# A hybrid decoder layer with 32 experts: writes moved to GpSimd's queue, two more fixed experts, two layer norms and two embeddings moved

## The chip, the cores and the metric

The kernel runs on one core of one Trainium2 chip. The metric is the device time of one execution in microseconds, as the median of several runs. A core has five engines with instruction streams of their own: TensorE (PE in the profile, its weight loads PEld), VectorE (DVE), ScalarE (ACT), GpSimd (POOL) and SyncE (SP), which only issues transfers. SyncE, ScalarE and GpSimd issue DMAs, and 16 DMA engines carry them.

## What is computed

One layer on 512 tokens of width 2048, all in float32:

```python
z = x @ w_in + b_in
y = concat(s5_group(z[:, :1024]), conformer_conv_group(z[:, 1024:2048], z[:, 2048:])) @ w_o + b_o
h = layer_norm(ALPHA * x + y, ln1_g, ln1_b)
# experts: 4 groups of 8; the best group, and in it the best 2 experts of each token
g_p, g_idx = top_k(softmax(h @ w_rg + b_rg), 1)
e_val, e_idx = top_k((h @ w_re + b_re)[the 8 of group g_idx], 2)
w = softmax(e_val) * g_p
m = sum over a token's 2 experts of (silu(h @ w_gate[e]) * (h @ w_up[e]) * w) @ w_down[e]
h = layer_norm(ALPHA * h + m, ln2_g, ln2_b)
e = (p @ w_p) * sigmoid(h @ w_pg + b_pg)        # p: a second input, 512 x 256
out = layer_norm(ALPHA * h + e, ln3_g, ln3_b)
```

An expert has 6 MB of weights (2048 x 512 for gate and up, 256 x 2048 for down), so 32 experts have 201 MB.

## The kernel before

The program is written as straight Python that unrolls every loop. A planner (`schedule_with_timeline_sim=True`) then decides the order of the instructions on each engine: it simulates the engines, and whenever one is free gives it the ready instruction that stands earliest in the code. So an instruction that stands late can run early if it is ready in a gap. Engines then run their own stream strictly in that order. The planner also places the semaphores. For the transfers of SyncE and ScalarE together it has eight, used in turn; a transfer waits until the one that used its semaphore before it has landed. GpSimd's transfers have eight of their own.

Tokens are worked on in four tiles of 128 (`m`, `NT` = 4). The stages that matter here are these.

The *output projection* (line 880 on) makes `tt[m]`, a tile's 128 x 2048 sums, in four column blocks `c`. `evac` adds a block, takes its statistics, and `logits` transposes it and multiplies it with the routers' weights (lines 843 to 859). In the last block `finish(m)` (line 861) makes mean and 1/sigma of the tile, its router logits `lg[:, m]` (line 867), and, for all but the last tile, calls `normalize`: eight instructions on VectorE (lines 180 and 181) and the write of the tile to `h_dram` (line 877, ScalarE's queue). The last tile's `normalize` stands further down, behind the counts (line 961).

The *routing* (lines 915 to 1036) works on VectorE with small tiles: group and expert choice (to line 955), the tokens of each expert by matmuls with ones (lines 957 to 960), each expert's rank by its count (lines 973 to 979), each token's rank and position (`rtok`, line 991), a one-hot of positions (line 190, called from `slot_hot`), and from it the rows to gather (`sl0`, line 196) and the weights (`wt0`, line 203). Experts named in `FIXED` get the last ranks whatever their counts. `embedding(m, x)` (line 828) multiplies a tile of p with `w_p` and writes it to `p_dram` (line 841); its argument `x` only makes it wait for that tile. Before, `embedding(0)` waits for the last logits, `embedding(1)` for the largest overflow count and `embedding(2)` for `wt0`.

The *expert stage* (line 1046 on) goes through `GROUPS`. A group is one pass of 128 token slots: one to four experts, given by rank, share the slots in strips of 128, 64 or 32. For each group GpSimd gathers token rows from `h_dram` (`gather`), TensorE transposes them (`columns`), multiplies with gate and up in four quarters (`up`, line 1103), and with down in two halves (`down`, line 1123), and GpSimd scatters the result to `y_dram`. A quarter or half of an expert is one 1 MB load by `ring_load` (line 1065) into a ring of `NRING` = 17 slots: 15 tiles that are there from the start and, once `w_p` is no longer needed, the two `raw` buffers. An expert number that comes from the routing is read into a register of SyncE (line 1137); a fixed one is in the code. Group 0 is the fixed experts 0 and 31. Its 12 loads are issued first (`early`), then three loads of group 1, then the embedding of the last tile with its two buffers `pe` of which there is one at a time (lines 1171 to 1179), then two more loads of group 1 into the raw buffers. Then comes a branch for tokens that found no slot (line 1187, not taken here), at which every engine settles its semaphores, and then the other groups.

The *last stage* (line 1246 on) loads `w_pg`, adds the experts' rows from `y_dram` to `tt`, and makes the second and third layer norm and the gate with `p_dram`.

Of the kernel before, what the change touches and what calls it, by code (L numbers as in the profile page):

```python
# [8 lines left out]
FT = mybir.dt.float32  # L9
# [8 lines left out]
P = 128  # L18
# [8 lines left out]
NT = S // P  # L27
NE = 32
FH = 256
ALPHA = 2.0 ** 0.25  # L30
# [12 lines left out]
FIXED = (0, NE - 1)  # L43
GROUPS = [(64, [(30, 2), (31, 2)]), (128, [(0, 4)]), (32, [(2, 3), (13, 1)]), (128, [(1, 4)]),
# [10 lines left out]
def build(tc, I, out, dbg=None, stages=9):  # L55
# [582 lines left out]
    if True:  # L638
# [146 lines left out]
        with ExitStack() as s3:  # L785
# [42 lines left out]
            def embedding(m, x):  # L828
# [5 lines left out]
                for q in range(2):  # L834
                    pe_ = wB.tile([P, 2, 512], FT, name="pe", tag="wlo", bufs=4)
                    for c in range(2):
                        ps = bank("ops")
                        for k in range(2):
                            T.matmul(ps, pm[:, k], wps[q][:, k, c * 512:(c + 1) * 512], start=k == 0, stop=k == 1)
                        A.copy(pe_[:, c], ps)  # L840
                    A.dma_start(p_dram[m, 2 * q:2 * q + 2].rearrange("c p d -> p c d"), pe_)
# [19 lines left out]
            def finish(m):  # L861
                mean, rstd = ln_stats(op_, st1[m], "s")
                nm = op_.tile([P, 1], FT, name="nm", bufs=2)
# [4 lines left out]
                if m < NT - 1:  # L868
                    normalize(m, mean, rstd)
                return mean, rstd  # L870

            def normalize(m, mean, rstd):
# [4 lines left out]
                A.dma_start(h_dram[m * P:(m + 1) * P], tt[m])  # L877
                dump("h", tt[m], lambda d: d[m * P:(m + 1) * P])

            for c in range(4):  # L880
# [19 lines left out]
                else:  # L900
                    hls = [next(w_o) for q in range(2)]
                    for m in range(NT):
# [3 lines left out]
                        last = finish(m)  # L906
# [5 lines left out]
            embedding(0, lg[:, NT - 1, 0:1])  # L912
# [48 lines left out]
            normalize(NT - 1, *last)  # L961
# [29 lines left out]
            V.tensor_reduce(rtok, pt2, axis=AX.X, op=OP.add)  # L991
            by_place, pw = rp1.tile([P, 2 * NT, NP], FT), rp.tile([P, 2 * NT, NP], FT)
# [44 lines left out]
            embedding(1, cmax)  # L1037
            embedding(2, wt0[:, 0:1])
# [8 lines left out]
    if True:  # L1047
# [84 lines left out]
        def expert(i, j):  # L1132
            if i == 0:
                return slice(FIXED[j], FIXED[j] + 1)
# [13 lines left out]
        pm3 = ep.tile([P, 2, P], FT, name="pm3")  # L1148
        nc.sync.dma_start(pm3, I["pT"][:, :, (NT - 1) * P:])
        for m in range(NT):  # L1150
            A.mul(tt[m], tt[m], ALPHA)
# [3 lines left out]
        for i, (width, members) in enumerate(GROUPS):  # L1155
# [4 lines left out]
            for q in range(4):  # L1160
                up(gu, st, early[q] if i == 0 else ahead1[q] if i == 1 else loads(i, q), q)
# [3 lines left out]
            for q in range(2):  # L1165
                down(at, st, early[4 + q] if i == 0 else ahead1[4] if (i, q) == (1, 0) else loads(i, 4 + q), q, sl0[:, NGR + i:NGR + i + 1])
# [3 lines left out]
            ahead1 = [loads(1, q) for q in range(3)]  # L1170

            for q in range(2):
                pe_ = ep.tile([P, 2, 512], FT, name="pe")
                for c in range(2):
                    ps = bank("dps", 4)
                    for k in range(2):
                        T.matmul(ps, pm3[:, k], wps[q][:, k, c * 512:(c + 1) * 512], start=k == 0, stop=k == 1)
                    (A.copy if c else V.tensor_copy)(pe_[:, c], ps)
                A.dma_start(p_dram[NT - 1, 2 * q:2 * q + 2].rearrange("c p d -> p c d"), pe_)
            ring.extend(rpool.tile([P, D], FT, name="raw", tag="raw", bufs=2) for _ in range(2))  # L1180
            ahead1 += [loads(1, q) for q in range(3, 5)]
# [282 lines left out]
```

## Time and profile before

| what | us |
|---|---|
| median of 3 runs (1479.26 to 1485.14) | 1480.44 |
| the profiled execution, whole | 1482.75 |
| its span, first to last instruction | 1480.9 |
| TensorE busy | 1262.3 (85%) |
| VectorE busy | 778.5 (53%) |
| ScalarE busy | 372.5 (25%) |
| GpSimd busy | 382.7 (26%) |

The mean granted TensorE clock was 0.926. 349.34 MB went through the DMA, 236 GB/s over the span. The profile gives, for one execution, each instruction with its start, its duration and what ended the idle time before it; DMA packets; and a chain of waits followed back from the last instruction. Times are from the span's start. "q" behind an engine's name marks its sequencer, which waits, branches and issues transfers.

### The profile page before, as it was taken

How to read it: one execution, taken by the hardware profiler on the slowest of the kernel's cores; microseconds unless marked ns; L12 is line 12 of the kernel's file. 1: busy time of each engine (PE TensorE's matmuls, PEld its weight loads, DVE VectorE, ACT ScalarE, POOL GpSimd, SP SyncE). 2: the span in 40 equal slices, each digit the busy share in tenths (PEclk: the TensorE clock that was granted, in tenths of full speed). 3: DMA queues.
4: the chain of work that ended last, by engine and by line, in shares of the span. 5: the costliest groups of instructions: out<-in, count | busy, mean ns of one | idle time of the engine just before them, and what ended most of it. 6: DMA issues, size and time to landing. Idle time of an engine off the chain costs nothing. (4 is left out here: it accounts for less than half of the span.)

```text
span 1480.9 us, 16676 instructions
## 1 busy us (share of the span) xinstructions
PE 1262.3 (85%) x6206; PEld 805.9 (54%) x6207; DVE 778.5 (53%) x1251; ACT 372.5 (25%) x559; POOL 382.7 (26%) x313
## 2 busy tenths in 40 slices
PE   6999999998999999968598998777676775599996
PEld 4887877887777888844243332221111111388884
DVE  7999899879998653681111110000000006985467
ACT  4335565544433432031001110000000003023210
POOL 0367768673945300000001111000000005700000
PEclk9998999998999999978899999898899986699998
DMA  6344445445632351147799999999999986426413
GB/s 233 112 131 118 150 122 156 142 117 174 246 123 85 114 210 57 44 170 284 298 422 420 420 420 416 418 417 414 415 411 411 411 351 235 142 107 213 142 44 121
DMA packets 97769, 349.34 MB, mean 236 GB/s; under 512 B 29705, under 2 KB 43529, under 8 KB 62097
## 3 DMA queue, kind: packets, MB, share of 16 engines
q1 hardware_dynamic: 51152, 303.21, 52.7%
q10 hardware_dynamic: 40912, 28.20, 6.6%
q0 software_dynamic: 5616, 16.79, 2.9%
q8 instruction: 51, 0.84, 0.2%
q14 instruction: 38, 0.30, 0.1%
HBM read 323.30 MB, written 35.34 MB: 242 GB/s over the span
## 5 line engine op out<-in xcount | busy, mean ns | idle before, releaser
L1103 PE MATMUL gu<-ring,xt 128*32 128x512 f32 (+2 forms) x1144 | 237.9, 671 | 58.7 <-DMA ring<-w_gu 58.7
L236 DVE SCALAR_TENSOR_TENSOR cps<-hc,wdw,cps 128x512 f32<-128x512 f32 x232 | 174.5, 752 | 4.8
L1103 PEld LDWEIGHTS gu<-ring,xt 128*32 128x32 f32 (+2 forms) x1144 | 58.7, 127 | 200.2 <-issue 100.2
L100 PE MATMUL zp<-xh,whi 128*128 128x512 f32 x384 | 157.5, 411 | 11.3 <-ACT whi L79 10.2
L79 ACT CAST whi<-raw 128x1024 fp32r<-128x1024 f32 x116 | 119.5, 1049 | 169.7 <-PE zp L102 55.7
L102 PE MATMUL zp<-xh,wlo 128*128 128x512 f32 x384 | 155.2, 404 | 1.5 <-DVE wlo L80 1.5
L101 PE MATMUL zp<-xl,whi 128*128 128x512 f32 x384 | 154.9, 403 | 1.6 <-DVE xl L80 1.6
L80 DVE TENSOR_TENSOR wlo<-raw,whi 128x1024 fp32r<-128x1024 f32 x90 | 123.8, 1386 | 55.3 <-ACT whi L79 54.4
L1109 DVE TENSOR_TENSOR act<-act,gu 128x256 f32<-128x256 f32 x13 | 5.5, 421 | 268.9 <-ACT act L1108 268.9
L1123 PE MATMUL dps<-ring,at 128*32 128x512 f32 (+2 forms) x568 | 113.6, 612 | 12.1 <-DMA ring<-w_dn 7.0
L1073 POOL DMA_INDIRECT y_dram<-ob,sl x26 | 25.6, 985 | 367.6 <-ACT ob L1125 358.0
L80 POOL TENSOR_TENSOR wlo<-raw,whi 128x1024 fp32r<-128x1024 f32 x26 | 72.4, 2787 | 85.8 <-ACT whi L79 73.3
L100 PE MATMUL fps<-whi,h2h 128*128 128x512 f32 x224 | 89.2, 399 | 0.7 <-ACT h2h L79 0.7
L102 PE MATMUL fps<-whi,h2l 128*128 128x512 f32 x224 | 89.3, 399 | 0.0
L100 PEld LDWEIGHTS zp<-xh,whi 128*128 128x128 f32 x384 | 74.6, 194 | 26.0 <-ACT whi L79 10.3
L101 PE MATMUL fps<-wlo,h2h 128*128 128x512 f32 x224 | 88.7, 397 | 0.0
L102 PEld LDWEIGHTS zp<-xh,wlo 128*128 128x128 f32 x384 | 74.6, 194 | 18.2 <-DVE wlo L80 2.4
L101 PEld LDWEIGHTS zp<-xl,whi 128*128 128x128 f32 x384 | 74.6, 194 | 16.8 <-DVE xl L80 2.0
L1123 PEld LDWEIGHTS dps<-ring,at 128*32 128x32 f32 (+2 forms) x568 | 31.7, 120 | 81.8 <-issue 54.5
L1125 DVE COPY ob<-dps 128x512 f32<-128x512 f32 x26 | 18.0, 692 | 108.5 <-PE dps L1123 108.5
L1088 DVE COPY xt<-xtp 128x512 f32<-128x512 f32 x26 | 18.0, 692 | 107.5 <-PE xtp L1083 107.5
L1069 POOL DMA_INDIRECT gx<-h_dram,sl x13 | 13.7, 1052 | 195.9 <-PE xtp L1083 133.2
(449 smaller groups left out, 2306.2 us busy)
## 6 DMA issues: line engine op xcount, KB each, us to landing
ring<-w_gu SPq DMA_DIRECT2D x114, 1024.0 KB
ring<-w_dn SPq DMA_DIRECT2D x56, 1024.0 KB
raw<-w_in SPq DMA_DIRECT2D x24, 1024.0 KB
raw<-w_o SPq DMA_DIRECT2D x16, 1024.0 KB
raw<-w_gu SPq DMA_DIRECT2D x14, 1024.0 KB
raw<-w_pg SPq DMA_DIRECT2D x14, 1024.0 KB
raw<-w_dn SPq DMA_DIRECT2D x8, 1024.0 KB
raw<-y_dram SPq DMA_DIRECT2D x12, 512.0 KB
```

Source lines behind the costliest of these rows:

```text
L79: A.copy(hi, src)
L80: eng.tensor_tensor(lo, src, hi.bitcast(FT), op=OP.subtract)
L100: T.matmul(ps, lh, rh, start=start, stop=False)
L101: T.matmul(ps, lh, rl, start=False, stop=False)
L102: T.matmul(ps, ll, rh, start=False, stop=stop)
L236: V.scalar_tensor_tensor(ps if k < 30 else acc, hc[:, k:k + S], wdw[:, ct, k:k + 1], ps, op0=OP.mult, op1=OP.add)
L1069: G.indirect_dma_start(out=gx, out_offset=None, in_=h_dram, in_offset=bass.IndirectOffsetOnAxis(ap=ig, axis=0), bounds_check=S - 1, oob_is ...
L1073: G.indirect_dma_start(out=y_dram[q], out_offset=bass.IndirectOffsetOnAxis(ap=isc, axis=0), in_=ob[:, q * 1024:(q + 1) * 1024], in_offset= ...
L1088: V.tensor_copy(o, ps)
L1103: T.matmul(gu[cols], xt[:, k, cols], raws[j][:, kk * 512:(kk + 1) * 512], start=k == 0, stop=k == KD - 1)
L1123: T.matmul(outs[c][cols], at[:, k, cols], raws[j][:, o:o + 512], start=k == 0, stop=k == 1)
L1125: (A.copy if c else V.tensor_copy)(ob[:, q * 1024 + c * 512:q * 1024 + (c + 1) * 512], outs[c])
```

## The change

Writes to `h_dram` and `p_dram` are issued by GpSimd instead of ScalarE. Two more experts are fixed (15 and 16), and they make up a second group of their own, so that there are 14 groups. Ahead of the branch 16 loads are issued instead of 17: group 0's twelve and two quarters of group 1. `normalize` of tile 2 moves behind the counts, beside that of tile 3. `embedding(0)` waits for `rtok`, `embedding(1)` for `wt0`, and the embeddings of tiles 2 and 3 are both in the expert stage. The scaling of `tt` by ALPHA on ScalarE moves behind them.

```diff
-FIXED = (0, NE - 1)
-GROUPS = [(64, [(30, 2), (31, 2)]), (128, [(0, 4)]), (32, [(2, 3), (13, 1)]), (128, [(1, 4)]),
-          (32, [(3, 3), (14, 1)]), (64, [(5, 2), (6, 2)]), (32, [(4, 3), (15, 1)]), (64, [(7, 2), (8, 2)]),
-          (32, [(9, 2), (11, 1), (12, 1)]), (32, [(10, 2), (16, 1), (17, 1)]), (32, [(18, 1), (19, 1), (20, 1), (21, 1)]),
-          (32, [(22, 1), (23, 1), (24, 1), (25, 1)]), (32, [(26, 1), (27, 1), (28, 1), (29, 1)])]
+FIXED = (0, NE - 1, NE // 2 - 1, NE // 2)
+GROUPS = [(64, [(28, 2), (29, 2)]), (64, [(30, 2), (31, 2)]), (128, [(0, 4)]), (32, [(2, 3), (11, 1)]), (128, [(1, 4)]),
+          (32, [(3, 3), (12, 1)]), (64, [(5, 2), (6, 2)]), (32, [(4, 3), (13, 1)]), (64, [(7, 2), (8, 2)]),
+          (64, [(9, 2), (10, 2)]), (32, [(14, 1), (15, 1), (16, 1), (17, 1)]), (32, [(18, 1), (19, 1), (20, 1), (21, 1)]),
+          (32, [(22, 1), (23, 1), (24, 1), (25, 1)]), (64, [(26, 2), (27, 2)])]
...
-                    A.dma_start(p_dram[m, 2 * q:2 * q + 2].rearrange("c p d -> p c d"), pe_)
+                    G.dma_start(p_dram[m, 2 * q:2 * q + 2].rearrange("c p d -> p c d"), pe_)
...
-                if m < NT - 1:
+                if m < NT - 2:
                     normalize(m, mean, rstd)
-                return mean, rstd
+                return m, mean, rstd
...
-                A.dma_start(h_dram[m * P:(m + 1) * P], tt[m])
+                G.dma_start(h_dram[m * P:(m + 1) * P], tt[m])
...
-            embedding(0, lg[:, NT - 1, 0:1])
...
                 T.matmul(cn[:, 0:NE], ones, oh[:, j], start=j == 0, stop=j == NT - 1)
-            normalize(NT - 1, *last)
+            for d in done[NT - 2:]:
+                normalize(*d)
...
             V.tensor_reduce(rtok, pt2, axis=AX.X, op=OP.add)
+            embedding(0, rtok[:, 0:1])
...
-            embedding(1, cmax)
-            embedding(2, wt0[:, 0:1])
+            embedding(1, wt0[:, 0:1])
...
-            if i == 0:
-                return slice(FIXED[j], FIXED[j] + 1)
+            if i < 2:
+                return slice(FIXED[2 * i + j], FIXED[2 * i + j] + 1)
...
-        pm3 = ep.tile([P, 2, P], FT, name="pm3")
-        nc.sync.dma_start(pm3, I["pT"][:, :, (NT - 1) * P:])
-        for m in range(NT):
-            A.mul(tt[m], tt[m], ALPHA)
+        pm = ep.tile([P, 2, 2 * P], FT, name="pm")
+        nc.sync.dma_start(pm, I["pT"][:, :, 2 * P:])
...
-            ahead1 = [loads(1, q) for q in range(3)]
-            for q in range(2):
-                pe_ = ep.tile([P, 2, 512], FT, name="pe")
-                for c in range(2):
-                    ps = bank("dps", 4)
-                    for k in range(2):
-                        T.matmul(ps, pm3[:, k], wps[q][:, k, c * 512:(c + 1) * 512], start=k == 0, stop=k == 1)
-                    (A.copy if c else V.tensor_copy)(pe_[:, c], ps)
-                A.dma_start(p_dram[NT - 1, 2 * q:2 * q + 2].rearrange("c p d -> p c d"), pe_)
+            ahead1 = [loads(1, 0)]
+            for m in range(2):
+                for q in range(2):
+                    pe_ = ep.tile([P, 2, 512], FT, name="pe")
+                    for c in range(2):
+                        ps = bank("dps", 4)
+                        for k in range(2):
+                            T.matmul(ps, pm[:, k, m * P:(m + 1) * P], wps[q][:, k, c * 512:(c + 1) * 512], start=k == 0, stop=k == 1)
+                        (A.copy if c else V.tensor_copy)(pe_[:, c], ps)
+                    G.dma_start(p_dram[2 + m, 2 * q:2 * q + 2].rearrange("c p d -> p c d"), pe_)
+            for m in range(NT):
+                A.mul(tt[m], tt[m], ALPHA)
             ring.extend(rpool.tile([P, D], FT, name="raw", tag="raw", bufs=2) for _ in range(2))
-            ahead1 += [loads(1, q) for q in range(3, 5)]
+            ahead1.append(loads(1, 1))
```

## Rows read from the trace of the kernel before

**Rows 1.** The page: GB/s in 40 slices; GpSimd's DMA queue (packets, MB).

```profile
GB/s 233 112 131 118 150 122 156 142 117 174 246 123 85 114 210 57 44 170 284 298 422 420 420 420 416 418 417 414 415 411 411 411 351 235 142 107 213 142 44 121
...
q0 software_dynamic: 5616, 16.79, 2.9%
```

**Rows 2.** Busy us of PE, PEld, DVE, ACT, POOL by stretch; clock, DMA share.

```profile
632.00:647.60 15.60, 7.21 (x35) 6.75 (x34) 15.51 (x50) 2.98 (x3) 0.00 (x0) 0.59 0.32 134
717.00:734.00 17.00, 8.65 (x24) 3.24 (x20) 2.00 (x3) 1.76 (x3) 2.09 (x3) 0.89 0.58 197
780.00:1000.00 220.00, 185.83 (x1100) 62.20 (x1094) 25.35 (x42) 21.71 (x42) 21.05 (x21) 0.96 1.01 419
```

**Rows 3.** The chain that ended last, end of the expert stage (start, us, what).

```profile
1207.39 20.50 DMA ring<-w_dn
...
1227.93 2.85 PE dps L1123 x16
1230.79 0.33 SPq L1265
```

**Rows 4.** SyncE in order of time, 699 to 735 us (start, us, instruction).

```profile
699.84 1.51 SPq L1065 DMA_DIRECT2D ring<-w_gu  x3
...
725.68 0.33 SPq L1065 DMA_DIRECT2D raw<-w_dn  x1
734.25 0.35 SPq L1065 DMA_DIRECT2D ring<-w_dn  x1
```

**Rows 5.** What SyncE waited for, 600 to 740 us (total us, times, longest).

```profile
SPq L1065 <- DMA h_dram<-tt: 49.0, 1, 49.0
SPq L1065 <- DMA p_dram<-pe: 34.9, 6, 9.5
...
SPq L1187 <- SPq L1187: 7.4, 3, 5.2
```

**Rows 6.** VectorE in order of time, 646 to 671 us.

```profile
646.47 0.75 DVE L181 SCALAR_TENSOR_TENSOR tt<-tt,lny,ln_b 128x512 f32<-128x512 f32 x1
...
653.06 0.29 DVE L955 TENSOR_TENSOR scr<-scr 128x128 f32<-128x128 f32 x1
...
660.05 0.15 DVE L973 COPY scr<-zp 32x1 f32<-32x1 f32 x1 [3.75 <-PE zp L958]
...
663.63 0.40 DVE L991 TENSOR_REDUCE scr<-scr 128x8 f32<-128x256 f32 x1
...
669.26 1.23 DVE L190 TENSOR_TENSOR rsc<-iof,scr 128x1024 f32<-128x1024 f32 x1
```

**Rows 7.** TensorE in order of time, 649 to 740 us.

```profile
649.98 6.25 PE L839 MATMUL zp<-raw,pm 128*128 128x512 f32 x8 [4.13 <-ACT pm L833]
...
659.60 0.41 PE L958 MATMUL zp<-ones,scr 128*32 128x1 f32 x8
...
677.41 1.86 PE L196 MATMUL cps<-rsc 128*128 128x26 f32 x16
...
682.12 8.83 PE L839 MATMUL zp<-raw,pm 128*128 128x512 f32 x16 [1.06 <-ACT pm L833]
691.62 0.66 PE L1083 MATMUL xtp<-ident,gx 128*128 128x128 f32 x4 [0.68 <-ACT pe L840]
...
718.52 7.13 PE L1177 MATMUL dps<-raw,pm 128*128 128x512 f32 x16
739.18 1.09 PE L1083 MATMUL xtp<-ident,gx 128*128 128x128 f32 x4 [13.53 <-DMA gx<-h_dram,sl]
```

**Rows 8.** Transfers that GpSimd writes to y_dram (0.5 MB each), issue to landing.

```profile
DMA to landing us min/median/max: 3.8/8.5/10.2
```

**Rows 9.** VectorE, 730 to 731 us: the second copy into the embedding's buffer.

```profile
730.90 0.69 DVE L1178 COPY pe<-dps 128x512 f32<-128x512 f32 x1 [9.66 <-DMA p_dram<-pe]
```

**Rows 10.** ScalarE: the activation of group 1 and that of group 6.

```profile
757.74 0.38 ACT L1108 ACTIVATE act<-gu 128x256 f32<-128x256 f32 x1 [6.23 <-PE gu L1103]
...
896.83 0.38 ACT L1108 ACTIVATE act<-gu 128x256 f32<-128x256 f32 x1 [6.42 <-PE gu L1103]
```

More of the change, by code (lines that the diff above doesn't have):

```diff
@@ L862, in finish @@
                 mean, rstd = ln_stats(op_, st1[m], "s")
-                nm = op_.tile([P, 1], FT, name="nm", bufs=2)
+                nm = op_.tile([P, 1], FT, name="nm", bufs=1)
                 V.scalar_tensor_tensor(nm, mean, -1.0, rstd, op0=OP.mult, op1=OP.mult)
@@ L900, in build @@
                 else:
+                    done = []
                     hls = [next(w_o) for q in range(2)]
@@ L905, in build @@
                         evac(m)
-                        last = finish(m)
+                        done.append(finish(m))
             pT = wB.tile([P, 2, S], FT, name="pT", tag="whi", bufs=4)
@@ L1160, in build @@
             for q in range(4):
-                up(gu, st, early[q] if i == 0 else ahead1[q] if i == 1 else loads(i, q), q)
+                up(gu, st, early[q] if i == 0 else ahead1[q] if i == 1 and q < 2 else loads(i, q), q)
             at = act(gu, wt0[:, i:i + 1])
@@ L1165, in build @@
             for q in range(2):
-                down(at, st, early[4 + q] if i == 0 else ahead1[4] if (i, q) == (1, 0) else loads(i, 4 + q), q, sl0[:, NGR + i:NGR + i + 1])
+                down(at, st, early[4 + q] if i == 0 else loads(i, 4 + q), q, sl0[:, NGR + i:NGR + i + 1])
             if i:
                 continue
-            ahead1 = [loads(1, q) for q in range(3)]
-            for q in range(2):
-                pe_ = ep.tile([P, 2, 512], FT, name="pe")
-                for c in range(2):
-                    ps = bank("dps", 4)
-                    for k in range(2):
-                        T.matmul(ps, pm3[:, k], wps[q][:, k, c * 512:(c + 1) * 512], start=k == 0, stop=k == 1)
-                    (A.copy if c else V.tensor_copy)(pe_[:, c], ps)
-                A.dma_start(p_dram[NT - 1, 2 * q:2 * q + 2].rearrange("c p d -> p c d"), pe_)
+            ahead1 = [loads(1, 0)]
[10 more added lines that the diff above has]
+                A.mul(tt[m], tt[m], ALPHA)
             ring.extend(rpool.tile([P, D], FT, name="raw", tag="raw", bufs=2) for _ in range(2))
-            ahead1 += [loads(1, q) for q in range(3, 5)]
+            ahead1.append(loads(1, 1))
             mo = xt[:, 0, 0:1].bitcast(I32)
```

## The prediction

> **What bounds the kernel now.** I read the 40 slices of the page first. The reader should see one flat stretch there, slices 21 to 32, with the DMA at 411 to 422 GB/s, and in front of it a ramp of 44, 170, 284 and 298 [rows 1]. The flat stretch is the expert stage. It loads 32 experts of six 1 MB blocks, 192 loads, whatever the routing says. By stretches the DMA engines are full at 419 GB/s from 780 to 1000 us while TensorE is busy 185.83 of 220; just ahead, from 717 to 734 us, they are only 0.58 busy [rows 2]. The chain that ended last runs through these loads: the last is issued at 1207.39, lands after 20.50, TensorE finishes with it, and at 1230.79 the last stage begins [rows 3]. So the end is: the moment from which loads flow without a break, plus the loads left, plus a fixed last stage of some 253 us.
>
> That moment is 734.25 us [rows 4]. Seventeen loads are out before it, because the ring has 17 slots. After load 17 (725.68) SyncE goes through the overflow branch at line 1187 and issues nothing for 8.57 us; among its waits is one of 5.2 [rows 4, 5]. The other 175 loads take 734.25 to 1227.93, which is 493.7 us or 2.82 each, gathers and scatters included.
>
> Ahead of the restart two chains run. One is SyncE's: its loads waited 49.0 us for an h_dram write and 34.9 us for p_dram writes [rows 5], because each weight load needs the semaphore of a transfer eight places earlier in the order of SyncE's and ScalarE's transfers, and those eight were ScalarE's writes. The other is the routing: logits, counts, slots, the gather of group 0 (TensorE starts on it at 691.62), its matmuls, then the embedding of the last 128 tokens at 718.52 [rows 7], whose weights sit in the two raw slots that loads 16 and 17 need.
>
> **The change, part by part.** *Writes on GpSimd, and four fixed experts.* The first seven loads no longer wait for ScalarE's writes, and all 24 loads of groups 0 and 1 need no routing (12 before). This brings loads forward, but it moves the end by nothing: no load beyond the 17th can leave before slots come free and SyncE is past the branch, and load 17 is already landed then. The change prefetches one block fewer (16, since only two quarters of group 1 are loaded ahead): +2.8 us.
>
> *Embedding 0 behind rtok.* Now its matmuls run from 649.98 and keep TensorE until the counts at 659.60, though the counts' input (line 955) is done at 653.35 [rows 6, 7]. Freed, the counts run at 653.4, and VectorE could go on 0.45 us later, as now at 660.05; it still has small work until 656.3 (3.75 idle before 660.05). I take 4 us off (between 3.7 and 5.0). *Embedding 1 is no longer in front of the slot rows.* Now those matmuls (line 196) start at 677.41 although the one-hot was ready at 670.49 [rows 6, 7]. Embedding 0 takes that place, but starts 0.9 us after rtok (line 991, done 664.03) and lasts 8.8 to 9.6 us, by the two embeddings of before [rows 7]. With rtok at 660.0 it ends at about 670.1: 7.3 us before 677.41, both moves together. Embedding 1 stands where embedding 2 stood (8.83 us before the first transpose), so group 0 starts 7.3 us earlier, at 684.3.
>
> *Two layer norms behind the count.* I give this nothing. The norm of the last tile already stands behind the count in the code, and VectorE still ran its last instruction at 646.47, ahead of the routing: the planner fills gaps with whatever is ready [rows 6]. Tile 2 will be drawn forward alike. The ends: if both stay behind the count, the last logits come sooner (from 632 to 647.6 us TensorE, which makes them, is busy 7.21 of 15.6 and VectorE 15.51 [rows 2], so I allow 6 us), but sixteen instructions of about 0.7 us then stand before the ranks. That is 6 us better to 3 us worse.
>
> *The embedding of two tiles in the expert stage.* It is 32 matmuls of 7.13/16 us instead of 16. Load 16, the last before the branch, needs the third quarter done, 10.7 us after group 0, where load 17 needed the second, 7.13 us after. So +3.5 us. From that issue to the restart I take 7 us instead of 8.57, since only one load is then in flight (between 5.7, the branch alone, and 8.6). Restart: 684.3 + 26.9 (691.62 to 718.52) + 10.7 + 0.2 + 7 = 729.1, which is 5.1 us sooner. Behind SyncE's wait for load 16 stand the branch and all later loads.
>
> *The writes of these quarters* go through one buffer, so each copy waits for the landing before it. Now there is one such wait. With the change there are three, and ScalarE, VectorE and the gather of group 1 stand behind them. The trace has no plain write from GpSimd. Nearest are its 0.5 MB scatters: 3.8, median 8.5, up to 10.2 us [rows 8]. I take 4.5 (DMA nearly idle), 6 (beside load 16) and 8.5 (after the restart). First copies end at 684.3 + 26.9 + 4.2 = 715.4; the last copy starts at 715.4 + 19.0 + 2 x 0.8 = 736.0. From such a copy (730.90) to TensorE's start on group 1 (739.18) it is now 8.3 us [rows 7, 9], so group 1 starts at 744.3 instead of 739.18.
>
> Does that late start cost? TensorE's groups come every (896.83 - 757.74)/5 = 27.8 us while it is behind [rows 10]. After group 4, with 48 loads used, load 66 waits for the first quarter of group 5. That path ends at 744.3 + 4 x 27.8 + 5 + 127 x 2.82 = 1218.6. The path of the loads alone ends at 729.1 + 176 x 2.82 = 1225.4, so the late start is hidden behind the loads with 6.8 us to spare.
>
> *Fourteen groups instead of thirteen.* They move no more bytes: GpSimd's queue moved 16.79 MB [rows 1], which is 1024 token rows of 8 KB gathered and scattered, so empty rows aren't moved. The extra 27.8 us of TensorE lie inside the stage in which it has idle time [rows 2]. The reference's routing on its inputs gives ranks 0 to 11 124, 98, 95, 93, 69, 64, 59, 38, 36, 29, 29, 26 tokens and the fixed experts 39, 19, 38, 15, all within their slots, so the overflow branch stays untaken.
>
> *The last stage.* The last group has 12 loads, so the small load at 1230.79 [rows 3] finds its slot free after the fifth quarter, up to 5 us sooner. The last scatter still ends last, so I take 1 us (0 to 5). The scaling of h, moved on ScalarE, is off every path, since ScalarE was busy 1.76 of 17 us there [rows 2].
>
> **Sum:** -5.1 + 2.8 - 1.0 = -3.3 us. The profiled execution took 1482.75 us (span 1480.9), so it would become 1479.4. The median of the runs shown is 1480.44, 2.3 us under that execution, and the forecast goes from it: 1477.
>
> **The rivals.** *Slower: the writes hold the branch.* At the branch an engine waits for the transfers that it issued, as SyncE does at line 1187 [rows 5]; if all four writes take 10.2 us and the gather waits for the fourth too, group 1 starts at 715.4 + 4 x 10.2 + 3 x 0.8 + 8.3 = 766.9, and TensorE's path ends at 1241.2, 13.3 us later than now: 1480.44 + 13.3 - 1.0 = 1493. It decides once group 1 starts after 751.1. For it speaks the 8.5 us median [rows 8]; against it, that the DMA is idle for the first two.
>
> *Faster: the planner pulls the new embedding forward.* If three quarters are done in the gaps of group 0, load 16 is issued at the end of group 0 and the restart is 684.3 + 26.9 + 0.2 + 7 = 718.4, 10.7 us sooner: 1466. For it speaks how far the last norm was drawn forward [rows 6]; against it, that the 16 matmuls of before stayed behind group 0 [rows 7].
>
> *No gain: routing isn't earlier.* If the norms stay behind the count, h of the last tile is written only at about 659, by GpSimd, while VectorE works without a pause (15.51 of 15.6 us in a stretch of before [rows 2]). If its descriptors wait until the one-hot's end at 670.5 and the write takes 10.2, it lands at 680.7, when the gather starts now. Then group 0 starts at 691.62 again: +7.3, 1484. The Trainium skill, SBUF — State Buffer, section "SBUF: two separate sides", states this hazard: a DMA issued from GpSimd can't get its descriptors written while VectorE holds the port that they share. No run here shows it for a plain write.
>
> **How the numbers follow.** Forecast 0.52 (its own range 1471 to 1483, from the ends of the norms and of the branch), slower rival 0.13, faster rival 0.20, no gain 0.15. The range 1466 to 1488 leaves out the slower rival and little else. Half a per cent is 7.4 us, about what a measurement of this kernel can tell from no change: faster (under 1473.0) 0.20 + 0.06 = 0.26; slower (over 1487.8) 0.13 + 0.02 = 0.15; the same 0.59.
>
> **What the profile after would show.** Seven ring loads issued before 640; counts at about 654; the slot rows at 670; TensorE on group 0 at 684; the first load after the branch at 729; group 1 between 742 and 751; the DMA flat from there. Norms of tiles 2 and 3 between counts and ranks would refute the planner's part. A ring that holds 16 landed loads while the DMA idles for over 10 us before the branch would show that the early loads bring nothing. I am wrong if the restart isn't what sets the end: if the DMA loses its flatness after it, TensorE has taken over.

## The result and the profile after

The changed kernel took 1491.18 us (median of 7 runs, 1487.09 to 1495.44) against 1482.35 us for the kernel before on the same chip (7 runs, 1479.26 to 1485.14). The ratio is 1.0058, 95% interval 1.0041 to 1.0075: slower by 8.6 us, more than half a per cent. The forecast was 1477 with a range to 1488, so direction and range were both wrong. The profiled execution has a span of 1489.4 us, 8.5 more than before, close to the difference of the medians.

The page first: GB/s in 40 slices, to be read beside [rows 1]. The ramp in front of the flat stretch is now 141, 260, 300, 273 (slices 18 to 21), and the flat part starts one slice later. GpSimd's queue moves 25.18 MB, the 8.4 MB of h and p more than before.

```profile
GB/s 233 110 131 119 152 145 136 144 113 217 219 122 57 114 209 57 227 141 260 300 273 420 417 400 421 421 421 418 419 411 415 417 359 203 141 99 219 140 44 120
...
q0 software_dynamic: 7776, 25.18, 4.3%
```

TensorE in order of time, for [rows 7]. The routing is as forecast or better: counts at 651.72, slot rows at 669.09 (forecast 654 and 670), and embedding 1 is through at 682.7. Then TensorE waits 10.01 us for the gather of group 0, and later 22.48 us for the gather of group 1.

```profile
651.72 0.59 PE L958 MATMUL zp<-ones,scr 128*32 128x1 f32 x8 [7.45 <-DVE scr L955]
...
669.09 1.97 PE L196 MATMUL cps<-rsc 128*128 128x28 f32 x16
...
680.85 1.88 PE L839 MATMUL xp<-raw,pm 128*128 128x512 f32 x4
692.74 1.08 PE L1084 MATMUL xtp<-ident,gx 128*128 128x128 f32 x4 [10.01 <-DMA gx<-h_dram,sl]
...
723.55 10.57 PE L1177 MATMUL dps<-raw,pm 128*128 128x512 f32 x24
...
762.46 1.09 PE L1084 MATMUL xtp<-ident,gx 128*128 128x128 f32 x4 [22.48 <-DMA gx<-h_dram,sl]
```

GpSimd in order of time shows why. It issues strictly in its order, and the gather of group 0 (686.47) stands behind the last write of embedding 1 (683.64) and a memset that ran at 628.81 before. The slot rows had been in SBUF since 671.7. The gather of group 1 (749.71) stands behind the fourth write of the new embedding.

```profile
683.64 0.72 POOL L841 DMA_DIRECT2D p_dram<-pe  x1 [2.72 <-ACT pe L840]
684.36 1.82 POOL L1129 MEMSET gx<- 128x2048 f32 x1
686.47 1.09 POOL L1070 DMA_INDIRECT gx<-h_dram,sl  x1 [0.29 <-POOL gx L1129]
...
728.17 0.79 POOL L1179 DMA_DIRECT2D p_dram<-pe  x1 [2.64 <-ACT pe L1178]
736.88 0.75 POOL L1179 DMA_DIRECT2D p_dram<-pe  x1 [7.92 <-DVE pe L1178]
742.80 0.71 POOL L1179 DMA_DIRECT2D p_dram<-pe  x1 [5.17 <-DVE pe L1178]
748.69 0.71 POOL L1179 DMA_DIRECT2D p_dram<-pe  x1 [5.18 <-ACTq L1189]
749.71 1.08 POOL L1070 DMA_INDIRECT gx<-h_dram,sl  x1 [0.31 <-issue]
```

SyncE in order of time, for [rows 4]. The first load after the branch is out at 748.40. Five loads go out up to 750.87. Then SyncE stands still until the sixth, at 771.36 (the second of the pair in the third line below): the ring is full, and its next slot is freed only by TensorE's late group 1.

```profile
734.15 6.19 SPq L1066 DMA_DIRECT2D raw<-w_gu  x2
748.40 2.27 SPq L1066 DMA_DIRECT2D ring<-w_gu  x4
750.87 20.82 SPq L1066 DMA_DIRECT2D ring<-w_dn  x2
771.94 0.33 SPq L1066 DMA_DIRECT2D ring<-w_gu  x1
```

What SyncE waited for, from 600 to 800 us (total us, times, longest), for [rows 5]: the longest of its five waits for TensorE's gate-up matmuls is that one.

```profile
SPq L1066 <- PE gu L1104: 31.9, 5, 19.9
```

With it the DMA loses its flatness behind the restart, which is what the prediction had named as the sign that TensorE sets the end. Busy us of PE, PEld, DVE, ACT, POOL, then clock, DMA share and GB/s from 750 to 780 us, in the kernel before:

```profile
750.00:780.00 30.00, 27.31 (x123) 11.03 (x125) 3.67 (x6) 3.11 (x7) 3.02 (x3) 0.94 1.01 421
```

The same stretch of the change:

```profile
750.00:780.00 30.00, 16.76 (x68) 6.36 (x70) 1.38 (x2) 1.17 (x2) 1.81 (x2) 0.67 0.75 293
```

The chain that ended last, for [rows 3]. The last gate-up block lands at 1223.78; activation, transpose and all down matmuls come behind it.

```profile
749.71 12.62 DMA gx<-h_dram,sl
...
1223.78 3.66 PE gu L1104 x14
...
1229.84 6.34 PE dps L1124 x21
```

GpSimd in order of time, its last two scatters:

```profile
1236.18 0.97 POOL L1074 DMA_INDIRECT y_dram<-ob,sl  x1 [28.66 <-ACT ob L1126]
1239.62 0.97 POOL L1074 DMA_INDIRECT y_dram<-ob,sl  x1 [2.46 <-ACT ob L1126]
```

The last scatter before was at 1232.49. From it to the end of the span it was 248.4 us, now 249.8: the last stage is the same to 1.4 us, and 7.1 of the 8.5 us were lost before it.

### The profile page after: what moved, and what is told of

The parts are those of the page before. It is cut to its first block, busy times and chain, and to the rows that moved or that the text cites. A ratio compares the mean times of both kernels' runs of the same rounds, so it can differ in the third digit from the quotient of the medians.

```text
span 1489.4 us, 16537 instructions
## 1 busy us (share of the span) xinstructions
PE 1264.2 (85%) x6128; PEld 809.5 (54%) x6129; DVE 784.9 (53%) x1258; ACT 373.5 (25%) x562; POOL 394.9 (27%) x330
## 3 DMA queue, kind: packets, MB, share of 16 engines
q0 software_dynamic: 7776, 25.18, 4.3%
## 4 chain that ended last, share of the span: by engine, by line
PE 24%; DMA 19%; DVE 5%; issue 1%; ACT 1%; POOL 0%; DVEq 0%; SPq 0%; POOLq 0%
DMA ring<-w_gu 12%; PE gu L1104 7%; DMA ring<-w_dn 6%; PE dps L1124 4%; PE fps L102 3%; PE fps L100 3%; PE fps L101 3%; PE xtp L1084 1%; DMA gx<-h_dram,sl 1%; DVE tt L180 1%; DVE tt L181 1%; PE h2p L102 0%; PE h2p L100 0%; PE h2p L101 0%; DVE lnq L166 0%
## 5 line engine op out<-in xcount | busy, mean ns | idle before, releaser
L1104 PE MATMUL gu<-ring,xt 128*32 128x512 f32 (+2 forms) x1032 | 231.3, 634 | 42.6 <-DMA ring<-w_gu 42.6
L100 PE MATMUL zp<-xh,whi 128*128 128x512 f32 x384 | 157.7, 412 | 10.2 <-ACT whi L79 10.2
L1104 PEld LDWEIGHTS gu<-ring,xt 128*32 128x32 f32 (+2 forms) x1032 | 62.6, 129 | 176.7 <-issue 101.5
L1124 PE MATMUL dps<-ring,at 128*32 128x512 f32 (+2 forms) x584 | 132.3, 619 | 13.0 <-DMA ring<-w_dn 6.5
L1124 PEld LDWEIGHTS dps<-ring,at 128*32 128x32 f32 (+2 forms) x584 | 38.2, 128 | 91.6 <-issue 63.2
L100 PEld LDWEIGHTS zp<-xh,whi 128*128 128x128 f32 x384 | 73.5, 192 | 25.9 <-ACT whi L79 10.3
L1084 PE MATMUL xtp<-ident,gx 128*128 128x128 f32 x224 | 38.2, 296 | 44.3 <-DMA gx<-h_dram,sl 32.5
```

Of the source, the lines that this page charges most:

```text
L100: T.matmul(ps, lh, rh, start=start, stop=False)
L1084: T.transpose(ps[:, kk * P:(kk + 1) * P], gx[:, k * P:(k + 1) * P], ident)
L1104: T.matmul(gu[cols], xt[:, k, cols], raws[j][:, kk * 512:(kk + 1) * 512], start=k == 0, stop=k == KD - 1)
L1124: T.matmul(outs[c][cols], at[:, k, cols], raws[j][:, o:o + 512], start=k == 0, stop=k == 1)
```

## The experiments

Each edit is on the changed kernel unless it says otherwise. Times are medians, ratios are to the kernel before, with 95% intervals. Each trace is of one execution; where its time lies more than 2 us from the median, the text says so.

**All writes on ScalarE again.**

```diff
-                    G.dma_start(p_dram[m, 2 * q:2 * q + 2]...
+                    A.dma_start(p_dram[m, 2 * q:2 * q + 2]...
-                G.dma_start(h_dram[m * P:(m + 1) * P], tt[m])
+                A.dma_start(h_dram[m * P:(m + 1) * P], tt[m])
-                    G.dma_start(p_dram[2 + m, 2 * q:2 * q + 2]...
+                    A.dma_start(p_dram[2 + m, 2 * q:2 * q + 2]...
```

> The changed kernel with all writes to h and p on ScalarE's queue, as in the kernel before; four fixed experts, groups, norms and embeddings as changed. Theory: what made the change slower is the order on GpSimd's queue (group 0's gather behind embedding 1's writes, group 1's gather behind the fourth write and beside the released loads). Without it group 0 starts at about 684 and group 1's gather is issued when VectorE has passed the branch: 1479 to 1486, no slower than the kernel before by more than measurement. Rival: the late group 1 comes from the embedding of two tiles ahead of the branch, whatever the queue: 1487 to 1492.

1482.65 us, 1.0001 (0.9986 to 1.0017): the kernel before to within 2.5 us. So the loss of the change is in the queue of the writes, and its other parts together bring nothing that can be told. Group 0's gather goes out at 674.48 and TensorE starts on it at 685.45. Group 1 still starts late, at 758.35: its four writes took 10.6 to 12.8 us each beside the loads, and its gather, issued 1.4 us behind the first load after the branch, 10.3.

**Only the p writes of embeddings 0 and 1 on ScalarE.** The first two lines of that diff.

> The changed kernel with the p writes of embeddings 0 and 1 (routing stage) on ScalarE's queue again; all other writes stay on GpSimd. Theory: the gather of group 0 was issued at 686.47 only because it stood behind these writes in GpSimd's order, though the slot rows were ready at 671.7. Without them it is issued at about 674 and TensorE, held by embedding 1 until 682.7, starts group 0 at about 683 instead of 692.7; quarters, branch and group 1 follow 8 to 10 us earlier, the wait of the loads for a ring slot (19.9 us) shrinks by as much: 1482 to 1485. Rival: the weight loads wait for these writes' semaphores again and the ring fills later, so that group 0 starts no earlier or lacks its blocks: 1490 to 1492.

1485.82 us, 1.0023 (1.0006 to 1.0041), 5.2 us better than the change. GpSimd in order of time, the gather of group 0:

```profile
674.23 1.08 POOL L1070 DMA_INDIRECT gx<-h_dram,sl  x1 [25.29 <-DVE sl L199]
```

TensorE in order of time, group 0, the embedding behind it, and group 1:

```profile
684.14 0.60 PE L1084 MATMUL xtp<-ident,gx 128*128 128x128 f32 x4
...
711.01 10.57 PE L1177 MATMUL dps<-raw,pm 128*128 128x512 f32 x24
...
759.00 1.08 PE L1084 MATMUL xtp<-ident,gx 128*128 128x128 f32 x4 [27.92 <-DMA gx<-h_dram,sl]
```

Group 0 starts at 684.1, to 0.2 us what the prediction had, and its 26.9 us to line 1177 are those of before. So these writes alone made group 0 late. Group 1 gains only 3.5 us (759.00), since the four writes, the first of them earlier by 12.5 us, now run beside the loads and land later. The four writes of line 1179 here, issue to landing:

```profile
DMA to landing us min/median/max: 7.0/9.3/9.6
```

The same four in the change:

```profile
DMA to landing us min/median/max: 4.5/6.0/9.1
```

**The gather of group 1 ahead of the writes.** It goes out as soon as TensorE has read group 0's rows, and again inside the branch.

```diff
-            if i + 1 < NGR and i:
+            if i + 1 < NGR:
                 gather(sl0[:, i + 1:i + 2])
...
-            gather(sl0[:, 1:2])
+                gather(sl0[:, 1:2])
             columns()
```

> The changed kernel with the gather of group 1 issued as soon as TensorE has read the rows of group 0, ahead of the p writes (it is issued again inside the branch, which isn't taken). Theory: TensorE started on group 1 at 762.5, 14 us after the branch, only for this gather (issued 749.7 behind the fourth write, 12.6 us to landing beside six loads). With the rows there, group 1 starts at about 750, the wait of the loads for a ring slot falls from 19.9 to about 8 us, and the end comes 10 to 12 us earlier: 1479 to 1482. Rival: TensorE's late start is hidden by the loads, as the prediction had it, and the end doesn't move: 1489 to 1492.

1478.88 us, 0.9987 (0.9968 to 1.0006), 10.5 us better than the change. The trace is of an execution of 1475.31 us, 3.6 under this median. The gather leaves at 701.74, and in TensorE's order of time group 1 begins as soon as VectorE is past the branch:

```profile
744.32 1.09 PE L1084 MATMUL xtp<-ident,gx 128*128 128x128 f32 x4 [9.59 <-DVEq L1189]
```

Counted from the gather of group 0 (682.79 here, 686.47 in the change) group 1 starts 14.5 us earlier, and the longest wait for a slot is 6.5 us instead of 19.9. TensorE's late group 1 was not hidden.

**Two buffers for the copies of the new embedding.**

```diff
-                    pe_ = ep.tile([P, 2, 512], FT, name="pe")
+                    pe_ = ep.tile([P, 2, 512], FT, name="pe", bufs=2)
```

> The changed kernel with two buffers for the copies of the embedding in the expert stage instead of one. Theory: three landings stood one behind the other (7.4, 4.6 and 4.6 us from issue to landing) between the first copy and the fourth; with two buffers the third copy waits for the first landing only, so that the fourth write goes out 7 to 9 us sooner, and with it the branch and the gather of group 1; the wait of the loads for a slot shrinks as much: 1480 to 1485. Rival: two writes in flight beside the loads take twice as long each, or the branch waits for their landing anyway: 1488 to 1492.

1483.91 us, 1.0024 (1.0001 to 1.0046), 5.0 us better than the change, with 4 of uncertainty. Of its ten executions five took 1476.6 to 1481.7 us and five 1486.1 to 1489.5; the trace is of the shortest, 1476.57, so it shows what the edit can do, and what happened in the longer five is not shown. In this execution the gather of group 1 leaves at 743.09, four us ahead of the first load behind the branch (747.06), and TensorE starts at 748.94, 5.9 us after it. In the change, issued 1.3 us behind the first of five loads, it took 12.6 us. TensorE in order of time:

```profile
748.94 1.08 PE L1084 MATMUL xtp<-ident,gx 128*128 128x128 f32 x4 [11.90 <-DMA gx<-h_dram,sl]
```

**GpSimd's writes alone, on the kernel before.** Its three write lines, `A` to `G`.

> The kernel before with all writes to h and p on GpSimd's queue and nothing else changed. Theory: in GpSimd's order the gather of group 0 now stands behind the six p writes of the routing stage, the last of which can be issued only when embedding 2 is copied (ScalarE issued it at 691.6 in the kernel before, 10.8 us after the gather). The gather goes out at about 694 instead of 680.8, TensorE starts group 0 at 701 to 705 instead of 691.6, loads 16 and 17, the branch and group 1 follow: 1482 + 10 = 1492, between 1488 and 1497. Rival: the first weight loads no longer wait 84 us in all for ScalarE's writes, and this is worth more than the late gather: 1482 or less.

1497.83 us, 1.0127 (1.0083 to 1.0170): 18.8 us worse (12 to 25, from four executions), more than expected. The last write of embedding 2 and the memset hold the gather, and group 0 starts 11.5 us late, at 703.09. GpSimd in order of time:

```profile
689.96 0.72 POOL L841 DMA_DIRECT2D p_dram<-pe  x1 [2.72 <-ACT pe L840]
690.67 1.82 POOL L1128 MEMSET gx<- 128x2048 f32 x1
692.78 1.10 POOL L1069 DMA_INDIRECT gx<-h_dram,sl  x1 [0.29 <-POOL gx L1128]
```

The first load behind the branch follows at 748.88 instead of 734.25 and the last scatter at 1245.42 instead of 1232.49. That is 13 of the 18.8 us, and 13.1 is also what this execution (1495.85) took more than the profiled one before; the rest of the median's loss is not shown.

**Four fixed experts alone, on the kernel before.** `FIXED`, `GROUPS`, `expert` and `ahead1` as changed.

> The kernel before with the four fixed experts and fourteen groups alone (16 loads ahead of the branch in the code, one narrow buffer smaller so that it fits): writes, norms and embeddings as before. Theory: the planner draws all 24 loads of groups 0 and 1 ahead of the branch, as in the changed kernel, seven more than before, worth up to 7 x 2.82 = 19.7 us on the path of the loads; group 1 starts at about 739 as before, so TensorE keeps up; the shape of the last group costs 6.5. 1482.4 - 15 + 6.5 = 1474, between 1469 and 1480. Rival: loads ahead of the branch are worth nothing, since TensorE or the slots set the pace, and the last group's shape is all: 1487 to 1490.

1479.81 us, 0.9980 (0.9965 to 0.9995): 3.0 us better, where 8 had been expected. All 24 loads of groups 0 and 1 are out ahead of the branch. But SyncE waits at the branch until they have landed: the last of them, issued at 730.0, landed 19.9 us later, and the next load leaves at 750.61, 20.6 us after it, against 8.57 before [rows 4]. SyncE in order of time:

```profile
725.52 4.79 SPq L1065 DMA_DIRECT2D raw<-w_gu  x2
750.61 1.57 SPq L1065 DMA_DIRECT2D ring<-w_gu  x3
```

**Group 1's last eight loads behind the branch.** Their expert number is read from the routing again.

```diff
-        def expert(i, j):
-            if i < 2:
+        def expert(i, j, q):
+            if i == 0 or i == 1 and q < 2:
```

> The changed kernel, but the last two gate-up quarters and the down blocks of group 1 take their expert number from the routing again (it is the same number), so that these eight loads stay behind the branch and 16 go ahead of it, as the prediction had counted. Theory: the eight loads that the planner drew ahead of the branch were worth something: with 16 out at the branch the loads run without a pause from about 745, 176 of them x 2.82 = 1241 against 1228.8 now, so 10 to 15 us more: 1498 to 1506. Rival (the step of the prediction that early loads beyond the 16th bring nothing, because TensorE's late group 1 sets the end): 1489 to 1493.

1492.79 us, 1.0085 (1.0057 to 1.0112): 4.0 us worse than the change, with some 5 us of uncertainty, so it can't be told from it. The theory's 10 to 15 us are refuted; the time lies in the rival's range. The trace (of an execution 4.0 us above the median) does show the loads' path later, by the sum below 1240.3 instead of 1222.2. The branch was passed earlier (the second raw load, now the first behind it, leaves at 744.0), and TensorE's path ended at 1236.8 in the change anyway, so by that sum 3.5 us of it reach the end.

**The last group in strips of 32.**

```diff
-          (64, [(9, 2), (10, 2)]), (32, [(14, 1), ...]), (32, [(18, 1), ...]),
-          (32, [(22, 1), ...]), (64, [(26, 2), (27, 2)])]
+          (64, [(9, 2), (10, 2)]), (64, [(26, 2), (27, 2)]), (32, [(14, 1), ...]),
+          (32, [(18, 1), ...]), (32, [(22, 1), ...])]
```

> The changed kernel with the groups in another order: the last one is again four single experts in strips of 32 (24 loads, 8 of them down blocks) instead of two experts in strips of 64 (12 loads, 4 of them down blocks). Theory: with the changed kernel's order the last gate-up block lands at 1223.8, and the activation and 32 down matmuls still come behind it (to 1238.7), so the last scatter is issued 7.1 us later than before; with 8 down blocks behind the last gate-up block this hides again. 1491.2 - 6.5 = 1484.7, between 1483 and 1487, last scatter some 6 to 7 us earlier. Rival: the last loads land late because the loads stood still after the branch, and the shape of the last group is worth nothing: 1490 to 1492.

1489.58 us, 1.0054 (1.0036 to 1.0073). My theory falls: the shape of the last group is worth nothing that can be told. The last load now is a down block, and it lands at 1235.74, 12 us after the last gate-up block of the change; the loads as a whole were late. From the chain that ended last:

```profile
1214.97 20.73 DMA ring<-w_dn
1235.74 3.63 PE dps L1124 x20
```

**The norm of tile 2 in its old place.**

```diff
-                if m < NT - 2:
+                if m < NT - 1:
...
-            for d in done[NT - 2:]:
+            for d in done[NT - 1:]:
```

> The changed kernel with the layer norm of tile 2 back in its old place in the code, ahead of the counts. Theory (the step of the prediction that gave this move nothing): the planner draws the norm forward either way, so that VectorE's order differs by a few instructions inside the same stretch; no difference from the changed kernel, 1488 to 1494. Rival: with the norm behind the counts the logits and counts come sooner (they do come 1.7 us sooner than in the kernel before), so that undoing it costs 2 to 6 us: 1493 to 1497.

1488.02 us, 1.0039 (1.0010 to 1.0069). No loss from undoing the move; against the change it is 2.8 us less with 5 of uncertainty, so it can't be told from nothing (the profiled execution took 1493.37). In both kernels VectorE has the norms done before the routing.

**Three edits at once:** embedding writes on ScalarE, two buffers, early gather.

> Three edits on the changed kernel at once: the p writes of embeddings 0 and 1 on ScalarE, two buffers for the copies in the expert stage, the gather of group 1 right after TensorE has read group 0's rows. Theory: group 0 starts at 684 (as with the first edit alone), the fourth quarter is done at about 728, the first load after the branch goes out at 736 to 740 instead of 748.4 and TensorE starts group 1 at about 738 instead of 762.5, so that the loads never wait 20 us for a slot: 738 + 168 x 2.82 = 1212 for the last load against 1228.8, 1468 to 1476. Rival: the early group 0 is eaten by slower writes (10 us each when it was tried alone), so that the branch falls at 744 as before and the result is that of the early gather alone: 1477 to 1480.

1474.51 us, 0.9964 (0.9946 to 0.9983): 5.3 us better than before and 13.9 better than the change, the best of all and inside the theory's range. TensorE starts group 1 at 737.13. But the branch is passed no earlier than with the early gather alone (743.93), as the rival had it: SyncE's last load ahead of it leaves at 724.7, with the DMA 1.01 busy from 690 to 720 us, and its waits at the branch end only at 744.4. SyncE in order of time:

```profile
721.28 3.76 SPq L1066 DMA_DIRECT2D raw<-w_gu  x2
744.94 2.36 SPq L1066 DMA_DIRECT2D ring<-w_gu  x4
```

**The branch ahead of group 0**, with ScalarE's embedding writes and two buffers. With the branch out of the way, the gather and the transposes of group 1 also move to where the other groups have theirs, inside the group ahead:

```diff
+        with tc.If(most > 0):
+            ...
         gather(sl0[:, 0:1])
...
-            if i + 1 < NGR and i:
+            if i + 1 < NGR:
                 gather(sl0[:, i + 1:i + 2])
...
-            if i + 1 < NGR and i:
+            if i + 1 < NGR:
                 columns()
...
-            with tc.If(most > 0):
-                ...
-            gather(sl0[:, 1:2])
-            columns()
```

> The changed kernel with the p writes of embeddings 0 and 1 on ScalarE, two buffers for the copies in the expert stage, and the whole overflow branch moved ahead of the gather of group 0 (nothing else of the groups' order changes). Theory: what keeps the loads from flowing is the branch behind group 0, at which each engine waits until its own transfers have landed; ahead of group 0 only the early loads are in flight. Behind it the loads go on while group 0 runs; they stand still once more, until the third and fourth quarter have freed the two raw slots at about 731, with 22 landed: 731 + 170 x 2.82 = 1210 for the last load against 1219 with the three edits before: 1462 to 1469. Rival: group 0's gather now waits for the branch and the branch for early loads that land at 700, so that group 0 starts 15 us later and all is eaten: 1474 to 1482.

1490.10 us, 1.0055 (1.0035 to 1.0075). The theory falls, and the rival has the direction, though the time lies above its range too. Group 0's gather now waits for TensorE to pass the branch (684.08), and TensorE starts on it at 693.89, 10 us later than with the three edits. SyncE is held at the branch until its transfers have landed (707.51), and the register reads, some 16 us, follow with only three loads in flight. GpSimd in order of time:

```profile
684.08 1.08 POOL L1070 DMA_INDIRECT gx<-h_dram,sl  x1 [36.67 <-PEq L1154]
```

SyncE in order of time, the last transfer ahead of the branch and the first loads behind it:

```profile
690.25 0.66 SPq L1150 DMA_DIRECT2D pm<-pT  x1
707.51 18.75 SPq L1066 DMA_DIRECT2D ring<-w_gu  x6
```

Then TensorE waits for a block of group 1 in a raw slot, whose load left at 744 us or later. TensorE in order of time:

```profile
769.77 1.12 PE L1104 MATMUL gu<-raw,xt 128*64 128x512 f32 x1 [23.57 <-DMA raw<-w_gu]
```

**The same with the ring as a queue.**

```diff
-            t = ring[turn[0] % NRING]
-            turn[0] += 1
+            t = ring.pop(0)
+            ring.append(t)
```

> The kernel with the branch ahead of group 0's gather, and the ring served as a queue: the two raw slots are appended behind the fifteen others when the embedding is done with them, so that no load waits for them in turn (loads 16 and on take the slots that group 0 frees, from about 700). Theory: the loads flow without a pause from about 700, with 12 landed: 700 + 180 x 2.82 = 1208, TensorE's path from group 1 at about 731 ends at 1205: 1458 to 1466, a little below the branch's move alone. Rival: with two slots fewer in the first 30 loads TensorE sets the pace and it is no better than the branch's move alone.

1486.89 us, 1.0034 (1.0015 to 1.0053), far from 1458 to 1466. It is 3 us less than the branch's move alone with 4 of uncertainty, so the two can't be told apart, as the rival had it. The DMA is 0.75 busy from 720 to 750 us; the branch's drain and the register reads leave it part idle here too.

## Why the prediction was wrong

**Its two paths held; their inputs didn't.** The prediction took the later of the loads' path (first load behind the branch + loads left x 2.82) and TensorE's (start of group 1 + 474.3, that is 1218.6 - 744.3). With the times of each trace put in:

| kernel | loads ahead | first load behind branch | loads' path | group 1 starts | TensorE's path | last scatter |
|---|---|---|---|---|---|---|
| before | 17 | 734.25 | 1227.8 | 739.18 | 1213.5 | 1232.49 |
| change, as forecast | 16 | 729.1 | 1225.4 | 744.3 | 1218.6 | |
| change | 24 | 748.40 | 1222.2 | 762.46 | 1236.8 | 1239.62 |
| embedding writes on ScalarE | 24 | 744.37 | 1218.1 | 759.00 | 1233.3 | 1235.51 |
| early gather of group 1 | 24 | 743.93 | 1217.7 | 744.32 | 1218.6 | 1225.29 |
| two buffers | 24 | 747.06 | 1220.8 | 748.94 | 1223.3 | 1226.70 |
| three edits | 24 | 744.94 | 1218.7 | 737.13 | 1211.4 | 1223.52 |
| all writes on ScalarE | 24 | 746.55 | 1220.3 | 758.35 | 1232.7 | 1235.40 |
| eight loads behind the branch | 16 | 744.0 | 1240.3 | 759.72 | 1234.0 | 1246.53 |
| before + GpSimd's writes | 17 | 748.88 | 1242.4 | 758.42 | 1232.7 | 1245.42 |
| before + four fixed experts | 24 | 750.61 | 1224.4 | 749.06 | 1223.4 | 1230.20 |

The last scatter follows the later path by 2.2 to 6.7 us in all of them. Each row is one execution: those of the early gather and of the two buffers lie 3.6 and 7.3 us under their medians, that of the eight loads 4.0 above, the others within 2. The norm in its old place fits too (3 us behind TensorE's path), and the last group in strips of 32 comes 0.6 behind it. The two kernels with the branch ahead of group 0 are not in the table, because their loads do not flow without a break from the branch on. In the change TensorE's path decides, by 14.6 us. The prediction had named the point (group 1 later than 751.1) but put group 1 at 744.3, 18.2 us too early.

**The step that failed first** is "Embedding 1 stands where embedding 2 stood, so group 0 starts 7.3 us earlier, at 684.3". TensorE was free for it at 682.7. But moving a write to GpSimd's queue puts it in front of whatever that queue issues next, and that is the gather. The prediction priced the writes where they left (SyncE's semaphores) and in the expert stage, and passed over this place in the routing: 692.74, 8.4 us late. The run with ScalarE's embedding writes puts group 0 at 684.14, and GpSimd's writes alone on the kernel before cost 18.8 us.

**The step that decided** is "so the late start is hidden behind the loads with 6.8 us to spare", and it fails even with group 0 on time. In the run with ScalarE's embedding writes group 0 and line 1177 come as forecast, yet group 1 starts at 759.00, 14.7 us after the forecast, and TensorE's path ends 15.2 us after the loads'. There the writes of the quarters meet the loads: from the first copies to the start of the last it is 29.0 us instead of the 20.6 of the forecast, and from that copy to group 1 14.7 instead of 8.3. The early gather undoes this part alone: group 1 starts at 744.32, and the loss is gone.

**Terms of the same sum.** From group 0 to line 1177 it took 30.8 us instead of 26.9. TensorE had stood still for 10 us, and its granted clock from 690 to 720 us was 0.80, a mean between its two levels (1.2 and 2.4 GHz), where it had been 1.00 before and was 1.00 again with ScalarE's embedding writes. The other kernels agree: from group 0 to line 1177 it is 26.9 us in the five traces in which TensorE had work up to group 0, and 30.0 to 31.0 in the seven in which it had stood still for 9.8 to 14 us, those with the branch ahead of group 0 left out. The prediction had carried 26.9 over without asking what TensorE would be doing ahead of it. By stretches (PE, PEld, DVE, ACT, POOL busy, clock, DMA share, GB/s), the kernel before:

```profile
690.00:720.00 30.00, 26.55 (x121) 9.29 (x120) 3.83 (x7) 3.69 (x7) 1.51 (x2) 1.00 0.89 354
```

The same stretch of the change:

```profile
690.00:720.00 30.00, 24.46 (x98) 8.69 (x100) 3.13 (x6) 1.93 (x4) 0.00 (x0) 0.80 0.73 285
```

And with ScalarE's embedding writes:

```profile
690.00:720.00 30.00, 28.05 (x111) 10.38 (x110) 3.66 (x6) 3.10 (x6) 2.83 (x3) 1.00 0.96 378
```

The landings of the four quarters came out as sized: from the first copies (727.9) to the start of the last (747.46) it was 19.6 us, forecast 20.6. That is luck: they ran late, with the DMA 0.79 busy from 720 to 750 us, and with group 0 on time (0.91 busy) they took the 29.0 us above. From that copy to group 1 it was 15.0 us instead of 8.3, since the branch lets the first of five loads go 1.3 us ahead of the gather. So 8.4 + 4.0 (clock, first copies at 727.9 instead of 715.4) - 1.0 + 6.7 is, to rounding, the 18.2 us by which group 1 was late. These parts do not add up one by one: taking the 8.4 and the 4.0 away brought group 1 forward by 3.5.

**"One block fewer prefetched, 16: +2.8"** was wrong on the other side. A load with a fixed expert number isn't tied to the branch; the planner drew all of group 1 ahead of it, 24 loads. With 748.40 as its restart (19.3 us after the forecast) the loads' path still came 3 us before the forecast's. That such loads "move the end by nothing" is not true where the loads' path decides: on the kernel before, four fixed experts gave 3.0 us (0.7 to 5.2), where the sum had +2.8 for them. It is far less than the 19.7 us of seven loads, because SyncE waits at the branch for all that are in flight. In the change, where TensorE's path decides, eight loads put behind the branch cost 4.0 us with 5 of uncertainty, which can't be told from nothing.

**What held.** The norms behind the count: nothing. Counts and slot rows: within 2.3 us. Fourteen groups: the rows of the table with thirteen and with fourteen fit alike, to the 4.5 us in which they differ, with no term for the extra one. Seven ring loads were out by 640 us, and the norms ran ahead of the counts. The last stage was 1.4 us longer than before, where 0 to 5 less were expected; the shape of the last group, which I then suspected, didn't show.

**The rivals.** "The writes hold the branch" gave group 1 at 766.9 and 1493 us, close to 762.46 and 1491.2, but by other terms: the four writes landed after 4.5 to 9.1 us, not 10.2 each, and group 0's delay and the gather's transit made it up. With a chance of 0.13 it carried too little: the start of group 0, the 26.9 us behind it and the 8.3 us to group 1 had gone into TensorE's path as single times, with no worse end. "No gain" had group 0 at 691.6, near the 692.7 found, for a reason that the trace refutes: the norms did not stay behind the count, and the h writes of GpSimd landed in 4.1 to 6.3 us, the last two (4.2 and 4.1) issued while VectorE was busy 9.86 of 10 us. That the time came close is luck. The change by stretches, columns as above:

```profile
640.00:650.00 10.00, 1.89 (x8) 1.78 (x8) 9.86 (x47) 1.91 (x1) 1.07 (x2) 0.50 0.51 210
```

The transfers of line 877 in the change, issue to landing:

```profile
DMA to landing us min/median/max: 4.1/4.2/6.3
```

The hazard that the Trainium skill states (SBUF — State Buffer, section "SBUF: two separate sides") didn't show on these writes; the page ties it to certain VectorE instructions, and no run here tells whether those of the norms are among them. Another sentence of the Trainium skill (DMA: Bandwidth & Descriptors, section "Issuing engines are not separate DMA queues") says that issuing from several engines only saves the sequencer's time, since all transfers share the same 16 DMA engines. The traces fit this: group 1's gather took 12.6 us beside five loads in the change, and 5.7 ahead of them with two buffers. They add that the choice of the engine costs more than issue time where a later transfer waits in its order.

## What to carry to other kernels

Before moving a transfer to another engine's queue, write down what that queue issues next and when it has to go out; here two gathers on the critical path stood behind writes, and with the writes back on the other queue the loss was gone. A gather whose rows are ready belongs ahead of writes and of a branch, not behind them. When two paths end within a few us of each other, put the uncertainty of each of their inputs into the chances: here a margin of 7 us for one path became a lag of 15, and the kernel lost 8.6 us.

## What the runs showed that I had not expected

A branch costs what is in flight, not what was issued ahead of it. With four fixed experts on the kernel before, the last of 24 loads landed after 19.9 us and SyncE issued the next one 20.6 us after it. In the change 24 loads went ahead too, but the last landed after 5.4 us, and the next left 8.4 us after it, as in the kernel before with 17 (8.57). After 10 us without work TensorE's granted clock was 0.80 on the mean of 30 us, and from group 0 to line 1177 it took 3.9 us more. SyncE's reads of 28 expert numbers take 16 to 17 us, in which it issues no load. With the three edits the DMA stayed 1.01 busy meanwhile (694 to 711 us), on loads issued earlier; with the branch ahead of group 0 it was 0.53 busy (711 to 725 us).
